# Attention with both key blocks in one set of score columns, samples' values of both heads at once, and HGRN2 sums one step behind their products

## The chip, the cores and the metric

The kernel runs on one core of a Trainium2 chip. The metric is the device time of one execution in microseconds (us), as the median of several runs. Durations inside an execution come from one profiled run.

## What is computed

One inference step of two trunk layers. There is a prompt of 1024 tokens and there are 8 samples of 8 new tokens, 1088 tokens in all, of width 1024. Each layer projects the normalised input once and feeds three mixers, of which two matter here. The reference, cut:

```python
# (A) windowed attention: 8 query heads, 2 key heads, window 128
qb_len = WINDOW if t >= WINDOW else t
k_all = jnp.concatenate([buf_k, k], axis=1)        # buf: zeros for the prompt, a cache of 128 for samples
dist = WINDOW + np.arange(qb_len)[:, None] - np.arange(kb_len)[None, :]
valid = ((dist >= 0) & (dist < WINDOW))[None] & (k_pos >= 0)[:, None, :]
s = jnp.where(valid, s, MASK_VALUE)                # s: scaled q k, per query block of 128, 256 keys
m = jnp.maximum(jnp.max(s, axis=-1, keepdims=True), sink)
p = jnp.where(valid, jnp.exp(s - m), 0.0)
denom = jnp.sum(p, axis=-1, keepdims=True) + jnp.exp(sink - m)
o = jnp.einsum('bnkgqs,bnskd->bnqkgd', p / denom, v_blk)
# (C) HGRN2: per head of 128, gate f per token and channel, k = 1 - f
#     S = f * S + k i^T ;  o = q S     (exact per-token recurrence)
```

A query t of a block sees, of the block before, the keys i > t, and of its own block the keys i <= t. For each row of 256 scores exactly 128 are therefore valid, one in each column position modulo 128.

## The kernel before

**Staging.** Per layer the kernel runs through units of two 128-column slices of the input projection. Weights and activations are split into a high and a low part, and each product is three matmuls of one pass (lines 384 to 386 for channel-major outputs in groups of 24 matmuls over 384, 384 and 320 tokens; lines 403 to 405, and 410 and 411, for token-major outputs, 24 matmuls a group). The mixers are Python generators that stand in the list `side`. After each group `group_end` calls `pump`, which moves the first two generators of the list on by one step (by three steps where `NPA` is given: the gate units during attention). What a generator emits up to its next `yield` stands in program order behind that group and ahead of the next.

**Order on the engines.** GpSimd (POOL) and SyncE (SP) run in program order (`ORDERED`). TensorE (PE), VectorE (DVE) and ScalarE (ACT) are ordered by a planner, which takes program order as priority and, with its own estimates of durations, puts a later instruction ahead where it believes the earlier one not to be ready. Semaphores then hold the real dependences.

**Attention.** `attention` interleaves, for each of 8 query blocks n, `scores(n)` (three steps) with `values(n - 1)` (three steps); for n = 0 the second place is taken by `sample_attention`. In `scores`, each group of two query heads takes four score matmuls of up to 256 columns (line 846) into a bank `sc`; one fused VectorE operation per head (line 850) adds the mask, writes `P` and keeps the row maximum. `softmax` makes exponentials in place on ScalarE (line 767, with row sums) and scales by the reciprocal (line 771). In `values`, `P` is transposed on TensorE, 128 x 128 at a time (line 867, bank `pt`), copied out (lines 870 and 872) and multiplied with the values (line 880, bank `av`, one column half of the array for each key head).

**Samples.** The values of `sample_attention` (lines 962 and 964) are, for each of 8 samples and both key heads, one matmul of 32 columns over the 128 cached keys and one over the 64 new keys; line 967 copies the result `avs` out. A full-precision matmul (all but those split ones) leaves two records in the trace, a transpose one.

**HGRN2.** Each of the 4 heads is one `hgrn` generator; at most two run side by side with the projections. It takes token pairs by levels 1, 2, 4, ... 64. For levels 0, 1 and 2 the products of query and key are made elementwise on VectorE into the tile `e` (lines 509, 532 and 560) and summed over channels by matmuls with ones into the bank `dg` (lines 518, 521, 535 and 538); the sums are then laid into `A` by VectorE (lines 527, 544, 571). From level 4 on, line 582 and its like make the products on TensorE. Between levels VectorE scales Q (line 599) and GpSimd scales K (line 600). Later steps make states and outputs (`pos`, `dss`, `ds`, `po`), normalise on GpSimd (line 713) and transpose (`yt`, line 720). In the token-major units behind the heads, `b_consts` loads the spatial weights through SP and masks them on GpSimd (lines 994 and 995).

The tiles of 1152 columns come from one pool of 17 slabs; score, transpose and sum banks from one PSUM pool of four (`paux`), the projections' banks from another of four.

Of the kernel before, what the change touches and what calls it, by code (L numbers as in the profile page):

```python
# [10 lines left out]
F32 = mybir.dt.float32  # L11
# [14 lines left out]
NEG = -1e30  # L26
# [33 lines left out]
def _consts():  # L60
# [3 lines left out]
    i = np.arange(128)  # L64
    cur = np.where(i[None, :] <= i[:, None], f(0), f(NEG))
    prev = np.where(i[None, :] > i[:, None], f(0), f(NEG))
    c["mask_p"] = np.concatenate([prev, cur], 1).astype(f)
    ms = np.full((128, 2, 192), NEG, f)
# [82 lines left out]
def build(tc, i, o, L):  # L151
# [57 lines left out]
    def late_consts():  # L209
        late["mask_p"] = cst("mask_p", [128, 256])  # L210
        late["cos"] = cst("cos", [128, 9, 8])
        late["rot"] = cst("rot", [128, 2])
        late["sin"] = cst("sin", [128, 9, 8])
        late["blk"] = cst("blk", [64, 4])
        mask_h = cp.tile([128, len(MLEV), 64], U8, tag="mask_h", name="mask_h")
        mh = slab("mh")
        nc.sync.dma_start(v3(mh[:, 0:len(MLEV) * 64], 64), i["c_mask_h"])
        V.tensor_copy(mask_h, v3(mh[:, 0:len(MLEV) * 64], 64))
        late["mask_h"] = mask_h
        mask_2 = cp.tile([128, 2, 16], U8, tag="mask_2", name="mask_2")  # L220
        nc.sync.dma_start(v3(mh[:, 512:544], 16), i["c_mask_2"])
        V.tensor_copy(mask_2, v3(mh[:, 512:544], 16))
        late["mask_2"] = mask_2

    def rsqrt(v, out, w):
# [275 lines left out]
    def hgrn(l, h, f, q, v, spill):  # L501
# [7 lines left out]
        V.tensor_mul(e[:, 0:NTOK], q[:, 0:NTOK], K[:, 0:NTOK])  # L509
        yield  # L510
        A = slab("ha")
# [19 lines left out]
        two = lambda x, n: x[:, 0:n].rearrange("p (b two) -> p b two", two=2)  # L531
        V.tensor_mul(e[:, 0:NTOK // 2], two(Q, NTOK)[:, :, 1], two(K, NTOK)[:, :, 0])
        for j in range(4):
            r, w = slice(32 * j, 32 * j + 32), slice(16 * j, 16 * j + 16)
# [17 lines left out]
        for a, m in enumerate(LEV):  # L552
# [5 lines left out]
            if m == 2:  # L558
                four = lambda x: x[:, 0:NTOK].rearrange("p (b two m) -> p b two m", two=2, m=2)
                V.tensor_mul(e[:, 0:NTOK].rearrange("p (b t s) -> p b t s", t=2, s=2),  # L560
                             four(Q)[:, :, 1, :].unsqueeze(3).to_broadcast([128, NTOK // 4, 2, 2]),
                             four(K)[:, :, 0, :].unsqueeze(2).to_broadcast([128, NTOK // 4, 2, 2]))
                pd = bank("dg2")
                group_sums(pd)
# [239 lines left out]
    def attention(l, q, kk, v, spill):  # L804
# [25 lines left out]
        def scores(n, QS):  # L830

            w = 256 if n else 128
            k0 = (n - 1) * 128 if n else 0
            P = slab("P")
            P = (P, slab("P"), 0) if n else (P, P, 512)
            st["P", n] = lambda a, g, c=0, x=w: P[a][:, a * P[2] + g * w + c:a * P[2] + g * w + c + x]
            cols = st["P", n]
            mx = small("smx", 8)
            for a in range(2):
                for gp in range(2):  # L840
                    ps = bank("sc")
                    for j in range(2):
                        g = gp * 2 + j
                        lq = QS[:, a * 512 + g * 128:a * 512 + g * 128 + 128]
                        for hl in range(2):
                            T.matmul(ps[:, j * 256:j * 256 + w], lq, KS[a][hl][:, k0:k0 + w],
                                     start=hl == 0, stop=hl == 1)
                    for j in range(2):
                        g = gp * 2 + j
                        V.tensor_tensor_reduce(cols(a, g), ps[:, j * 256:j * 256 + w],  # L850
                                               late["mask_p"][:, 256 - w:256], 1.0, -3e38, ALU.add, ALU.max,
                                               mx[:, 4 * a + g:4 * a + g + 1])
                yield
# [3 lines left out]
        def values(n):  # L857

            cols = st.pop(("P", n))
            nh = 2 if n else 1  # L860
            PT = slab("PT")
            PT = (PT, slab("PT"), 0) if n else (PT, PT, 512)
            for a in range(2):
                for hb in range(nh):
                    pt = bank("pt")
                    for g in range(4):
                        T.transpose(pt[:, g * 128:g * 128 + 128], cols(a, g, hb * 128, 128), ident)
                    d = PT[a][:, a * PT[2] + hb * 512:a * PT[2] + hb * 512 + 512]
                    if hb == 0:
                        S.copy(d, pt)  # L870
                    else:
                        V.tensor_copy(d, pt)
                yield
            del cols
            po = bank("av")
# [38 lines left out]
    def sample_attention(l, q, kn, v, spill):  # L914
# [39 lines left out]
        V.tensor_copy(PT[0:64, 512:1024], pn[0:64, :])  # L954
        yield
        po = bank("avs")
        for b in range(8):
            c, jj = b // 2, b % 2
            for a in range(2):
                s = (2 * jj + a) * 128 + 32 * c  # L960
                d = po[64 * a:64 * a + 64, b * 32:b * 32 + 32]
                T.matmul(d, cv[:, b * 128 + 64 * a:b * 128 + 64 * a + 64], PT[:, s:s + 32],
                         start=True, stop=False, tile_position=(0, 64 * a))
                T.matmul(d, v[0:64, 1024 + 64 * a:1024 + 64 * a + 64], PT[0:64, 512 + s:512 + s + 32],
                         start=False, stop=True, tile_position=(0, 64 * a))
        ys = slab("yss")
        S.copy(ys[:, 0:256].rearrange("p (g b t) -> p g b t", g=4, b=8),
               po[:, 0:256].rearrange("p (b g t) -> p g b t", b=8, g=4))
        nc.gpsimd.dma_start(spill[:, :, 1024:1088].rearrange("g p t -> p g t"), v3(ys[:, 0:256], 64))
# [421 lines left out]
```

## Time and profile before

| | before |
|---|---|
| median of 3 runs | 2421.92 us (2421.01 to 2422.5) |
| the profiled execution | 2422.11 us |
| its span in the trace | 2420.3 us |
| TensorE matmuls busy | 2345.0 us, 97% |
| TensorE weight loads busy | 2232.1 us, 92% |
| VectorE busy | 1116.6 us, 46% |
| ScalarE busy | 737.1 us, 30% |
| GpSimd busy | 398.8 us, 16% |

The span is the time from the first to the last instruction of the trace. Matmuls overlap in the pipeline, so the cost of one is read from its start to the start of the next, not from its length. A granted clock of 1.00 is TensorE at 2.4 GHz, 0.50 at 1.2 GHz; a value between is a mean over a stretch that has both.

### The profile page before, as it was taken

How to read it: one execution, taken by the hardware profiler on the slowest of the kernel's cores; microseconds unless marked ns; L12 is line 12 of the kernel's file. 1: busy time of each engine (PE TensorE's matmuls, PEld its weight loads, DVE VectorE, ACT ScalarE, POOL GpSimd, SP SyncE). 2: the span in 40 equal slices, each digit the busy share in tenths (PEclk: the TensorE clock that was granted, in tenths of full speed). 3: DMA queues.
4: the chain of work that ended last, by engine and by line, in shares of the span. 5: the costliest groups of instructions: out<-in, count | busy, mean ns of one | idle time of the engine just before them, and what ended most of it. 6: DMA issues, size and time to landing. Idle time of an engine off the chain costs nothing. (4 is left out here: it accounts for less than half of the span.)

```text
span 2420.3 us, 44177 instructions
## 1 busy us (share of the span) xinstructions
PE 2345.0 (97%) x18230; PEld 2232.1 (92%) x18230; DVE 1116.6 (46%) x2765; ACT 737.1 (30%) x1890; POOL 398.8 (16%) x429
## 2 busy tenths in 40 slices
PE   6999999989999999999999999999999999999999
PEld 5899898978899998999999998988888999999999
DVE  6446638485341232223573476476644312223251
ACT  4335632324121221212333356223332212112130
POOL 3100004242020021011110010142320101211111
PEclk9999999999999999999999999999999999999999
DMA  7421110203131233421432221111122213112141
GB/s 275 134 79 63 62 44 28 88 23 96 45 133 53 85 116 110 139 81 54 134 97 71 79 70 45 53 56 64 46 84 92 90 40 114 53 45 84 40 152 48
DMA packets 91049, 197.57 MB, mean 82 GB/s; under 512 B 14368, under 2 KB 21664, under 8 KB 90816
## 3 DMA queue, kind: packets, MB, share of 16 engines
q1 hardware_dynamic: 79616, 156.20, 19.9%
q0 software_dynamic: 11232, 38.55, 4.4%
q8 instruction: 143, 2.34, 0.4%
q14 instruction: 58, 0.48, 0.1%
HBM read 158.13 MB, written 38.54 MB: 81 GB/s over the span
## 5 line engine op out<-in xcount | busy, mean ns | idle before, releaser
L384 PE MATMUL mm<-H,wh 128*128 128x384 f32 (+1 forms) x1872 | 620.6, 331 | 2.0 <-ACT gq L1277 1.2
L386 PE MATMUL mm<-H,wh 128*128 128x384 f32 (+1 forms) x1872 | 612.9, 327 | 0.0
L385 PE MATMUL mm<-H,wl 128*128 128x384 f32 (+1 forms) x1872 | 612.4, 327 | 0.0
L403 PE MATMUL mm<-wh,H 128*128 128x256 f32 x1408 | 408.9, 290 | 0.0
L404 PE MATMUL mm<-wl,H 128*128 128x256 f32 x1408 | 401.2, 285 | 0.0
L405 PE MATMUL mm<-wh,H 128*128 128x256 f32 x1408 | 400.7, 285 | 0.0
L384 PEld LDWEIGHTS mm<-H,wh 128*128 128x128 f32 x1872 | 352.7, 188 | 16.0 <-issue 10.8
L386 PEld LDWEIGHTS mm<-H,wh 128*128 128x128 f32 x1872 | 352.3, 188 | 2.0 <-issue 1.6
L385 PEld LDWEIGHTS mm<-H,wl 128*128 128x128 f32 x1872 | 352.6, 188 | 0.3 <-issue 0.2
L339 DVE TENSOR_TENSOR wl<-wr,wh 128x512 fp32r<-128x512 f32 x308 | 219.4, 754 | 200.0 <-ACT wh L338 194.9
L403 PEld LDWEIGHTS mm<-wh,H 128*128 128x128 f32 x1408 | 271.4, 193 | 7.5 <-issue 5.2
L405 PEld LDWEIGHTS mm<-wh,H 128*128 128x128 f32 x1408 | 271.4, 193 | 2.6 <-issue 2.6
L404 PEld LDWEIGHTS mm<-wl,H 128*128 128x128 f32 x1408 | 271.8, 193 | 0.7 <-issue 0.2
L338 ACT CAST wh<-wr 128x512 fp32r<-128x512 f32 x312 | 177.7, 618 | 261.7 <-PE mm L386 204.8
L1288 DVE TENSOR_TENSOR gq<-gq,mm 128x384 f32<-128x384 f32 (+1 forms) x96 | 50.5, 531 | 336.0 <-PE mm L386 336.0
L1277 ACT ACTIVATE gq<-mm 128x384 f32<-128x384 f32 x144 | 68.1, 473 | 423.7 <-PE mm L386 403.5
L386 PE MATMUL mm<-yl,wh 128*128 128x384 f32 (+1 forms) x576 | 186.2, 330 | 5.3 <-DVE yl L1258 5.3
L384 PE MATMUL mm<-yh,wh 128*128 128x384 f32 (+1 forms) x576 | 190.3, 330 | 0.0
L385 PE MATMUL mm<-yh,wl 128*128 128x384 f32 (+1 forms) x576 | 188.4, 327 | 0.0
L1289 POOL TENSOR_TENSOR mg<-mg,gq 128x384 f32<-128x384 f32 (+1 forms) x96 | 95.4, 997 | 466.3 <-DVE gq L1288 466.3
L386 PEld LDWEIGHTS mm<-yl,wh 128*128 128x128 f32 x576 | 108.5, 189 | 6.5 <-DVE yl L1258 6.2
L1286 DVE TENSOR_TENSOR mg<-gq,mm 128x384 f32<-128x384 f32 (+1 forms) x48 | 25.1, 531 | 188.7 <-PE mm L386 120.0
(372 smaller groups left out, 3515.1 us busy)
## 6 DMA issues: line engine op xcount, KB each, us to landing
wr<-in_w_in SPq DMA_DIRECT2D x248, 256.0 KB, 3.4
wr<-in_w_ada SPq DMA_DIRECT2D x64, 256.0 KB, 3.3
yr<-y SPq DMA_DIRECT2D x24, 544.0 KB, 4.5
wr<-in_w_br SPq DMA_DIRECT2D x48, 256.0 KB, 3.2
gr<-y SPq DMA_DIRECT2D x16, 544.0 KB, 5.2
wada<-in_w_ada SPq DMA_DIRECT2D x16, 512.0 KB, 8.5
wr<-in_w_out SPq DMA_DIRECT2D x32, 256.0 KB, 3.5
y<-gq POOLq DMA_DIRECT2D x32, 192.0 KB, 2.1
```

The lines of the kernel that those rows point to most:

```text
L338: S.copy(hi, raw)
L339: eng.tensor_sub(wl[:, k0:k0 + 4, off:off + 128], raw, hi.bitcast(F32))
L384: T.matmul(ps[:, 0:n], a, rh, start=k == 0, stop=False)
L385: T.matmul(ps[:, 0:n], b, rh, start=False, stop=False)
L386: T.matmul(ps[:, 0:n], a, rl, start=False, stop=k == kk - 1)
L403: T.matmul(ps[:, 0:256], a, wh[:, k, :], start=k == 0, stop=False)
L404: T.matmul(ps[:, 0:256], a, wl[:, k, :], start=False, stop=False)
L405: T.matmul(ps[:, 0:256], b, wh[:, k, :], start=False, stop=k == 7)
L1277: S.activation(sg[c], ps, AF.Sigmoid)
L1286: V.tensor_mul(merged[j][:, t0:t0 + n], sg[c], ps)
L1288: V.tensor_mul(sg[c], sg[c], ps)
L1289: G.tensor_add(merged[j][:, t0:t0 + n], merged[j][:, t0:t0 + n], sg[c])
```

## The change

Four edits. (1) `scores`: the score matmuls stay; ScalarE copies the own block's 128 columns of two heads into `P`, VectorE overwrites those columns where the key of the block before is the valid one (a predicated copy under the mask `old`; for block 0 it puts in a large negative number), and a VectorE reduction per four heads makes the maxima. `P` has 128 columns per head where it had 256. (2) `values`: one transpose per head where there were two for n > 0; VectorE multiplies the transposed bank by the mask `oldT` for the part that goes with the values of the block before, and subtracts that from the bank for the part of the own block. The constants change accordingly: `mask_p` goes, `oldT`, `old` and a column of the negative number come. (3) `sample_attention`: one matmul of 512 columns over the new keys for all samples and both heads, then one of 64 columns per sample over its cache with the weights of both heads; the half of the output that mixes heads is not read. Four copies take the result out. (4) `hgrn`: the `yield` between the first product and the memset of `A` is taken out; one is put behind the product of line 532 and one behind that of line 560, so that their sums begin the next step.

```diff
--- before.py
+++ after.py
@@ -62,9 +62,8 @@
     c = {}
     c["ident"] = np.eye(128, dtype=f)
     i = np.arange(128)
-    cur = np.where(i[None, :] <= i[:, None], f(0), f(NEG))
-    prev = np.where(i[None, :] > i[:, None], f(0), f(NEG))
-    c["mask_p"] = np.concatenate([prev, cur], 1).astype(f)
+    c["old"] = (i[None, :] > i[:, None]).astype(f)
+    c["oldT"] = (i[:, None] > i[None, :]).astype(f)
     ms = np.full((128, 2, 192), NEG, f)
     row = np.arange(128)
     cc, t = row // 32, row % 8
@@ -207,7 +206,9 @@
     late = {}
 
     def late_consts():
-        late["mask_p"] = cst("mask_p", [128, 256])
+        late["oldT"] = cst("oldT", [128, 128])
+        late["neg"] = cp.tile([128, 1], F32, tag="neg", name="neg")
+        V.memset(late["neg"], NEG)
         late["cos"] = cst("cos", [128, 9, 8])
         late["rot"] = cst("rot", [128, 2])
         late["sin"] = cst("sin", [128, 9, 8])
@@ -221,6 +222,10 @@
         nc.sync.dma_start(v3(mh[:, 512:544], 16), i["c_mask_2"])
         V.tensor_copy(mask_2, v3(mh[:, 512:544], 16))
         late["mask_2"] = mask_2
+        old = cp.tile([128, 128], U8, tag="old", name="old")
+        nc.sync.dma_start(mh[:, 640:768], i["c_old"])
+        V.tensor_copy(old, mh[:, 640:768])
+        late["old"] = old
 
     def rsqrt(v, out, w):
         y, r = out, out.shape[0]
@@ -507,7 +512,6 @@
         V.tensor_mul(Q[:, 0:NTOK], q[:, 0:NTOK], f[:, 0:NTOK])
         e = q
         V.tensor_mul(e[:, 0:NTOK], q[:, 0:NTOK], K[:, 0:NTOK])
-        yield
         A = slab("ha")
         G.memset(A[:, 0:NTOK], 0.0)
         yield
@@ -530,6 +534,7 @@
 
         two = lambda x, n: x[:, 0:n].rearrange("p (b two) -> p b two", two=2)
         V.tensor_mul(e[:, 0:NTOK // 2], two(Q, NTOK)[:, :, 1], two(K, NTOK)[:, :, 0])
+        yield
         for j in range(4):
             r, w = slice(32 * j, 32 * j + 32), slice(16 * j, 16 * j + 16)
             T.matmul(pd[r, 288:416], ones[:, 0:32], v3(e[:, 0:512], 64)[:, :, w],
@@ -560,6 +565,7 @@
                 V.tensor_mul(e[:, 0:NTOK].rearrange("p (b t s) -> p b t s", t=2, s=2),
                              four(Q)[:, :, 1, :].unsqueeze(3).to_broadcast([128, NTOK // 4, 2, 2]),
                              four(K)[:, :, 0, :].unsqueeze(2).to_broadcast([128, NTOK // 4, 2, 2]))
+                yield
                 pd = bank("dg2")
                 group_sums(pd)
                 for j in range(4):
@@ -829,12 +835,12 @@
 
         def scores(n, QS):
 
+
             w = 256 if n else 128
             k0 = (n - 1) * 128 if n else 0
             P = slab("P")
-            P = (P, slab("P"), 0) if n else (P, P, 512)
-            st["P", n] = lambda a, g, c=0, x=w: P[a][:, a * P[2] + g * w + c:a * P[2] + g * w + c + x]
-            cols = st["P", n]
+            st["P", n] = P
+            cols = lambda a, g: P[:, (4 * a + g) * 128:(4 * a + g) * 128 + 128]
             mx = small("smx", 8)
             for a in range(2):
                 for gp in range(2):
@@ -845,33 +851,36 @@
                         for hl in range(2):
                             T.matmul(ps[:, j * 256:j * 256 + w], lq, KS[a][hl][:, k0:k0 + w],
                                      start=hl == 0, stop=hl == 1)
-                    for j in range(2):
-                        g = gp * 2 + j
-                        V.tensor_tensor_reduce(cols(a, g), ps[:, j * 256:j * 256 + w],
-                                               late["mask_p"][:, 256 - w:256], 1.0, -3e38, ALU.add, ALU.max,
-                                               mx[:, 4 * a + g:4 * a + g + 1])
+                    d = v3(P[:, (4 * a + 2 * gp) * 128:(4 * a + 2 * gp) * 128 + 256], 128)
+                    sc = v3(ps, 256)
+                    S.copy(d, sc[:, :, w - 128:w])
+                    V.copy_predicated(d, bc_mid(late["old"], 2), sc[:, :, 0:128] if n else
+                                      late["neg"].unsqueeze(2).to_broadcast([128, 2, 128]))
+                V.tensor_reduce(mx[:, 4 * a:4 * a + 4], v3(P[:, a * 512:a * 512 + 512], 128), AX.X, ALU.max)
                 yield
             softmax(lambda e: cols(e // 4, e % 4), mx, sinkp[l], 8)
             yield
 
         def values(n):
 
-            cols = st.pop(("P", n))
+            P = st.pop(("P", n))
             nh = 2 if n else 1
             PT = slab("PT")
             PT = (PT, slab("PT"), 0) if n else (PT, PT, 512)
             for a in range(2):
-                for hb in range(nh):
-                    pt = bank("pt")
-                    for g in range(4):
-                        T.transpose(pt[:, g * 128:g * 128 + 128], cols(a, g, hb * 128, 128), ident)
-                    d = PT[a][:, a * PT[2] + hb * 512:a * PT[2] + hb * 512 + 512]
-                    if hb == 0:
-                        S.copy(d, pt)
-                    else:
-                        V.tensor_copy(d, pt)
+                pt = bank("pt")
+                for g in range(4):
+                    e = (4 * a + g) * 128
+                    T.transpose(pt[:, g * 128:g * 128 + 128], P[:, e:e + 128], ident)
+                d = PT[a][:, a * PT[2]:a * PT[2] + 512]
+                if n:
+                    e = PT[a][:, 512:1024]
+                    V.tensor_mul(v3(d, 128), v3(pt, 128), bc_mid(late["oldT"], 4))
+                    V.tensor_sub(e, pt, d)
+                else:
+                    S.copy(d, pt)
                 yield
-            del cols
+            del P
             po = bank("av")
             for hb in range(nh):
                 for a in range(2):
@@ -953,19 +962,21 @@
         S.copy(PT[:, 0:512], pt)
         V.tensor_copy(PT[0:64, 512:1024], pn[0:64, :])
         yield
+
         po = bank("avs")
+        T.matmul(po, v[0:64, 1024:1152], PT[0:64, 512:1024], start=True, stop=False)
+        cols = lambda x, c, jj: x.rearrange("p (jj a c r) -> p jj a c r", jj=2, a=2, c=4)[:, jj, :, c, :]
         for b in range(8):
             c, jj = b // 2, b % 2
-            for a in range(2):
-                s = (2 * jj + a) * 128 + 32 * c
-                d = po[64 * a:64 * a + 64, b * 32:b * 32 + 32]
-                T.matmul(d, cv[:, b * 128 + 64 * a:b * 128 + 64 * a + 64], PT[:, s:s + 32],
-                         start=True, stop=False, tile_position=(0, 64 * a))
-                T.matmul(d, v[0:64, 1024 + 64 * a:1024 + 64 * a + 64], PT[0:64, 512 + s:512 + s + 32],
-                         start=False, stop=True, tile_position=(0, 64 * a))
+            T.matmul(cols(po, c, jj), cv[:, b * 128:b * 128 + 128], cols(PT[:, 0:512], c, jj),
+                     start=False, stop=b == 7)
         ys = slab("yss")
-        S.copy(ys[:, 0:256].rearrange("p (g b t) -> p g b t", g=4, b=8),
-               po[:, 0:256].rearrange("p (b g t) -> p g b t", b=8, g=4))
+        for a in range(2):
+            r = slice(64 * a, 64 * a + 64)
+            for jj in range(2):
+                d = ys[r, 0:256].rearrange("p (g c jj t) -> p jj c g t", g=4, c=4, jj=2)[:, jj]
+                x = po[r].rearrange("p (jj a c g t) -> p jj a c g t", jj=2, a=2, c=4, g=4)[:, jj, a]
+                (S.copy if jj else V.tensor_copy)(d, x)
         nc.gpsimd.dma_start(spill[:, :, 1024:1088].rearrange("g p t -> p g t"), v3(ys[:, 0:256], 64))
```

## Rows read from the trace of the kernel before

**Rows 1.** The page's first part: busy time, share of the span and instructions of TensorE.

```profile
PE 2345.0 (97%) x18230; PEld 2232.1 (92%) x18230; DVE 1116.6 (46%) x2765; ACT 737.1 (30%) x1890; POOL 398.8 (16%) x429
```

**Rows 2.** The list of waits, TensorE: line, releaser: us in total, times, longest.

```profile
PE dg L518 <- DVE q L560: 8.9, 6, 2.0
PE dg L535 <- DVE q L532: 8.4, 6, 2.4
PE yt L720 <- POOL v L713: 7.7, 6, 3.3
```

**Rows 3.** Busy time by stretch: us, then each engine (count), granted clock, DMA share, GB/s.

```profile
187.16:196.19 9.03, 9.03 (x65) 7.40 (x64) 3.51 (x7) 2.26 (x4) 0.54 (x1) 0.73 0.23 78
196.19:201.60 5.41, 5.41 (x24) 5.41 (x24) 2.58 (x10) 3.35 (x6) 0.77 (x1) 0.50 0.10 24
1383.85:1392.13 8.28, 8.28 (x65) 6.79 (x65) 3.86 (x13) 2.34 (x7) 0.54 (x1) 0.84 0.18 51
1392.13:1396.03 3.90, 3.90 (x18) 3.90 (x17) 1.91 (x4) 3.50 (x6) 0.77 (x1) 0.50 0.16 38
```

**Rows 4.** The timeline around 187 us, samples' values: start, us, engine, line, shapes, count.

```profile
187.16 0.30 PE L962 MATMUL avs<-PTs,cv 128*64 128x32 f32 x2
...
187.40 0.30 PE L964 MATMUL avs<-PTs,ts 64*64 64x32 f32 x2
```

**Rows 5.** TensorE's timeline, stretches 626 to 628 and 546 to 547 us.

```profile
626.50 1.02 PE L1003 MATMUL pz<-vb,ws 128*128 128x512 f32 x2
627.45 0.32 PE L1006 MATMUL pzs<-vb,ws 64*64 64x64 f32 x2
...
545.98 1.06 PE L685 MATMUL ds<-v,kt 128*128 128x128 f32 x8
546.87 0.38 PE L636 MATMUL pk<-c_ident,hk 128*128 128x128 f32 x2
```

**Rows 6.** TensorE's timeline, 210 to 212 us, the prompt's value products.

```profile
210.43 1.08 PE L880 MATMUL av<-PT,ts 128*64 128x512 f32 x4
211.43 1.21 PE L846 MATMUL sc<-ks,qs 128*128 128x256 f32 x8
```

**Rows 7.** TensorE's timeline, 213 to 215 us, transposes of the prompt's weights.

```profile
213.51 1.04 PE L867 MATMUL pt<-c_ident,P 128*128 128x128 f32 x8
214.30 0.39 PE L385 MATMUL mm<-H,wl 128*128 128x320 f32 x1
```

**Rows 8.** Timeline of the first head, then the stretch of three matmul groups.

```profile
348.65 1.29 DVE L509 TENSOR_TENSOR q<-q,hk 128x1088 f32<-128x1088 f32 x1
...
354.93 0.65 PE L518 MATMUL dg<-q,ones 128*32 128x256 f32 x8
...
364.17 1.28 DVE L560 TENSOR_TENSOR q<-hq,hk 128x1088 f32<-128x1088 f32 x1
...
365.51 0.66 PE L518 MATMUL dg<-q,ones 128*32 128x256 f32 x8 [0.74 <-DVE q L560]
...
343.07:354.93 11.86, 11.86 (x74) 11.67 (x73) 6.04 (x8) 5.22 (x10) 0.00 (x0) 1.00 0.29 90
```

**Rows 9.** Busy time by stretch, as in rows 3, behind a wait for `yt`.

```profile
571.47:577.14 5.67, 5.67 (x22) 4.17 (x22) 5.67 (x17) 0.69 (x1) 1.40 (x2) 0.51 0.01 3
```

**Rows 10.** VectorE's groups by line and form: count, busy us, mean ns, idle before.

```profile
L850 DVE CUSTOM_DVE_ANT_0 P<-sc,c_mask_p 128x256 f32<-128x256 f32 x112 | 42.2, 418 | 5.9 <-PE sc L846 5.5
...
L872 DVE COPY PT<-pt 128x512 f32<-128x512 f32 x28 | 19.3, 688 | 8.0 <-PE pt L867 8.0
...
L544 DVE COPY_PREDICATED ha<-mask_h,dg 32x128 f32<-32x128 uint8 x32 | 14.0, 439 | 0.7
...
L737 DVE TENSOR_REDUCE rss<-rq 64x8 f32<-64x512 f32 x2 | 1.3, 670 | 0.0
```

**Rows 11.** Busy time by stretch, as in rows 3, the fullest slice of attention.

```profile
230.00:240.00 10.00, 9.99 (x72) 9.47 (x71) 9.36 (x27) 5.93 (x11) 1.08 (x2) 1.00 0.21 67
```

**Rows 12.** ScalarE's groups by line: count, busy us, mean ns, idle before.

```profile
L767 ACT ACTIVATE P<-P,snm 128x256 f32<-128x256 f32 (+1 forms) x128 | 61.7, 485 | 21.0 <-DVE snm L761 12.5 <-DVE ses L763 8.5
```

## The prediction

> **What bounds the kernel now.** I read the busy shares first: TensorE's matmuls cover 97% of the span, its weight loads nearly as much [rows 1]. The reader sees that no other engine is near that, so an edit counts by the TensorE time that it takes away, or by the idle time of TensorE that it closes; work of VectorE and ScalarE counts only where TensorE waits for it. Next the list of TensorE's waits [rows 2]: in HGRN2, `dg` products of line 518 wait 8.9 us for the product `e` of line 560, those of line 535 wait 8.4 us for line 532, and the transposes `yt` wait 7.7 us for GpSimd's scaling. The attention's scores and values wait so little that the list does not name them. Last the stretches in which the granted clock is at its lower level [rows 3, 9]: two of them begin inside the samples' value products, one behind a `yt` wait.
>
> **Samples' values.** Before, 32 small matmuls a layer (lines 962 and 964, two records each); their stretch takes 9.03 us in the first layer and 8.28 us in the second [rows 3], together 17.3 us. Each costs 0.24 us at the full clock although it has only 32 columns [rows 4]. In both stretches the clock falls from the 2.4 to the 1.2 GHz level part of the way (mean 0.73 and 0.84), and the work behind them runs at 0.50 for 5.41 and 3.90 us before it rises again [rows 3].
> After: one matmul of 512 columns and eight of 64 columns with 128x128 weights. The nearest price of the first is line 1003, 0.95 us from its start to the next line's [rows 5]. For the eight, four matmuls of 128 columns with full weights take 0.89 us, 0.22 each [rows 5]; those of 32 columns cost 0.24, so 64 columns should lie there too. That makes 0.95 + 8 x 0.22 = 2.7, of which overlap at the seams takes a little: 2.6 us a layer, bounds 2.1 (each of the eight at some 0.14, were the columns to count) and 3.5. Saved: 17.3 - 5.2 = 12.1 us. As dense work of 2.6 us follows and precedes full-rate matmuls I take it that the clock stays up; half of 5.41 + 3.90 us is 4.65 us more. Term: -16.8 us, and -10 if the clock falls all the same.
> The four evacuations in place of one (two on VectorE, two on ScalarE) come behind the last matmul and feed a DMA to DRAM that is read much later; I cost them at nothing.
> A rule of the Trainium skill speaks against this part: "TensorE: Matmul & The Clock Gate", Part 3 on packing small matmuls, says that outputs in different column groups run side by side, which full-width outputs give up. The rows of the prompt's values agree with it: two half-width matmuls of 512 columns take 1.00 us, as one full-width does [rows 5, 6]. The samples' rows do not: 0.24 us for each [rows 4]. Were they packed they would cost as 16, 3.8 us a layer, and the term without the clock would be 2.4 us; the measured stretch decides.
>
> **Prompt's values.** Both key blocks are now in one set of 128 columns, so a block n > 0 transposes 8 tiles and not 16. Per layer 7 x 8 = 56 transposes go, 112 in all. Eight take 0.79 us to the next line's start, 0.099 each [rows 7]. Term: -11.1 us, all of it on TensorE's path. The score products and the value products keep their count (the two masked halves of the transposed tile go in separately).
>
> **What the scores and values now ask of VectorE and ScalarE.** Removed: 112 fused mask-and-maximum operations of 256 columns, 42.2 us, and 28 copies, 19.3 us [rows 10], 61 us (block 0's 16 shorter ones left out). Added on VectorE: 64 predicated copies of 256 elements; the nearest row has 128 elements in 0.44 us [rows 10], so 0.44 to 0.88, 28 to 56 us; 32 reductions of 512 elements at 0.67 [rows 10], 21 us; 28 products and 28 differences of 512 elements out of PSUM at the 0.69 of the copy, 39 us. Net +27 to +55 us, less what the shorter scaling gives back. ScalarE gets 64 copies of 256 columns, loses 28 of 512, and its exponentials have half as many columns. In the busiest slice VectorE already works 9.36 of 10 us while TensorE loses nothing [rows 11], because other projections stand between the steps. I put +2 us of new waits here; 0 if the gaps hold it all, +20 if they do not.
> The constants add one load on SP's queue, ahead of the modulation weights, and a cast: at most +1, taken as 0.
>
> **HGRN2's order.** A step of a head is emitted after each group of 24 projection matmuls. Two steps are added (the products `e` of lines 532 and 560 now end a step, their sums begin the next) and one is removed (GpSimd's memset joins the first step). What the trace shows of the old order: line 560's product starts at 364.17 and takes 1.28 us, TensorE stands for 0.74 us and then begins line 518 at 365.51 [rows 8]. With a group between (three take 11.86 us [rows 8], so 4.0 us each) each wait of at most 2.4 us [rows 2] is covered. The removed step hits the first sums: line 509's product ends at 349.94, line 518 begins at 354.93 [rows 8], 5.0 us of slack; one group earlier leaves 1.0. At heads whose vector work is denser less is left, so I keep 4 us of the 17.3 us (8.9 + 8.4): term -13.3, bounds -4 and -17.3. TensorE's order is made by a planner that fills in projection matmuls where it believes a product to be late; where it already did, the yield changes little, hence the lower bound.
> One step more per head also moves the ends of the heads. In the old order the third head's normalisation falls just behind the spatial masks, whose products GpSimd makes; `yt` waits up to 3.3 us for line 713 [rows 2], and behind that TensorE runs 5.67 us at 0.51 [rows 9]. Counting the steps, that head's scaling is now emitted two groups after the masks. If so some 2.2 us of wait and half of 5.67 us go per layer, 10 us in all; as the order of the queues could bring it back I count 6. Against it stands the fourth head's state load: it is emitted after the masks' loads and the next weights on SP, so its users may wait 0 to 2 us per layer: +1.
> The heads still end in the second unit of `ub`, ahead of the point where all side work is run out, and by the count of tiles no more than 17 slabs are alive, as before.
>
> **Sum.** -16.8 - 11.1 + 2 - 13.3 - 6 + 1 = -44.2 us. The profiled execution took 2422.1 us (span 2420.3), the median of the runs is 2421.9, so they agree: 2377.9 us, 1.8% less.
>
> **Rivals.** A, VectorE binds in attention: for it speaks the slice at 9.36 of 10 [rows 11], against it that TensorE's list names neither `sc` nor `pt` nor `av`. Price 10 to 20 us: 2388 to 2398. B, the planner puts the sums back where they wait: what speaks for it is that the trace has sums standing amid a group, not at its end; only some 4 us of term -13.3 is kept, 2387, and with the `yt` wait kept too 2393. C, slower: the score banks are now freed only after a ScalarE copy, and that copy may stand behind a burst of eight exponentials, 8 x 0.485 = 3.9 us [rows 12]; the next scores then find no bank. At 3.9 us for each of 16 blocks that is +62 us, 2439; it decides the sign from 44.2 / 16 = 2.8 us a block. Against it: the exponentials get shorter, four banks serve, and the projections have banks of their own. "TensorE: Matmul & The Clock Gate" of the Trainium skill calls ScalarE's queue strict first-in first-out (its section on the 32x32 sub-arrays), which is what C needs; no row here shows a copy behind such a burst holding TensorE. D, better: the waits of HGRN2's `yt` all go, none come new, and predicated copies are cheap: -16.8 - 11.1 - 17.3 - 10 = -55.2, 2367, and with the samples' lower bound and a shorter first `yt` wait some 4 us less, 2363.
>
> **How the numbers follow.** Forecast 0.47 (its own range 2370 to 2386), A 0.2, B 0.15, D 0.1, C 0.05, and 0.03 for a sum of small losses that ends within 0.2% of before (some 5 us, about what a measurement tells from none). Leaving out C and the tails of A and D, the range is 2363 to 2399. Faster 0.92, same 0.03, slower 0.05.
>
> **What would show it.** After: a samples' value stretch near 2.6 us with the clock at 1.00 behind it; 128 `pt` transposes, not 240; line 518's and 535's waits under 5 us in all; `yt` under 4 us and no lower clock behind it; VectorE's busy time up by 20 to 55 us without a new wait of TensorE on `sc`, `pt` or `av`. Wrong it is made by waits on these three tiles, or by sums that wait for line 509 or 532.

## The result and the profile after

The changed kernel takes 2384.2 us (median; 2382.2 to 2388.0) against 2422.2 us: 0.9846 of the time before, 95% interval 0.9829 to 0.9863. That is 38 us less where the forecast was 44 less (2377.9), inside the range, with the sign as forecast. The profiled execution, the shortest of the four, took 2382.2 us with a span of 2380.1, which is 40.2 us under the span of before. Where terms are added up below, it is done against spans.

The page's first part answers [rows 1]:

```profile
PE 2310.4 (97%) x18026; PEld 2200.4 (92%) x18026; DVE 1121.3 (47%) x2639; ACT 730.8 (31%) x1928; POOL 396.4 (17%) x429
```

TensorE is still the bound. Of the 40.2 us, 34.6 left its busy time (2345.0 to 2310.4) and 5.6 its idle time (span less busy: 75.3 to 69.7). The forecast had it otherwise: it looked for some 16 of its 44 us in waits that end, and put in 3 us for new ones.

The list of TensorE's waits, answering [rows 2] (line, releaser: us in total, times, longest):

```profile
PE dg L522 <- DVE q L514: 6.1, 2, 3.0
...
PE dg L540 <- DVE q L536: 5.2, 2, 2.6
...
PE pts L959 <- DVE Ps L777: 3.2, 2, 1.6
PE yt L726 <- POOL v L719: 2.9, 2, 1.5
PE ds L691 <- DVE s L683: 2.7, 2, 1.6
PE dg L522 <- DVE q L565: 2.2, 2, 1.4
```

Line 522 is line 518 of before, 540 is 535, 726 is 720. Three waits are new. The first sums of a head (line 522, product of line 514) stand once in each layer for 3.0 us: this is where the removed step struck. The samples' transposes (line 959) wait 1.6 us a layer for the samples' softmax. And the products `ds` of line 691 wait 2.7 us in all for VectorE's addition to the state (line 683). By the code they read nothing that line 683 writes; that they wait for a PSUM bank that it reads is likely, but no run shows it. None of the three attention tiles that the forecast feared (`sc`, `pt`, `av`) is listed.

The stretches that answer [rows 3] and [rows 9] (us, then each engine's busy time with its count, granted clock, DMA share, GB/s):

```profile
188.81:191.69 2.88, 2.88 (x20) 2.12 (x20) 2.34 (x11) 2.81 (x8) 0.00 (x0) 1.00 0.00 0
191.69:196.00 4.31, 4.31 (x33) 4.28 (x32) 4.15 (x9) 3.53 (x9) 1.31 (x2) 1.00 0.35 100
1364.50:1367.40 2.90, 2.90 (x19) 2.14 (x20) 1.88 (x10) 2.83 (x10) 0.00 (x0) 1.00 0.00 0
...
571.00:577.00 6.00, 6.00 (x54) 6.00 (x53) 0.30 (x1) 2.60 (x13) 0.54 (x1) 1.00 0.13 50
370.30:372.30 2.00, 2.00 (x9) 2.00 (x9) 1.93 (x8) 0.00 (x0) 0.00 (x0) 0.51 0.00 0
1672.90:1676.30 3.40, 3.40 (x44) 3.11 (x43) 3.24 (x8) 2.56 (x6) 1.32 (x2) 0.52 0.01 2
```

The samples' values take 2.88 and 2.90 us in place of 9.03 and 8.28, with the clock at 1.00 (the 2.4 GHz level) in and behind them. In the timeline the wide product (line 967) takes 1.06 us to the start of the next line, and the eight narrow ones (line 971) 1.83 us, 0.23 each:

```profile
188.75 1.12 PE L967 MATMUL avs<-PTs,ts 64*128 64x512 f32 x2
189.81 2.00 PE L971 MATMUL avs<-PTs,cv 128*128 128x64 f32 x16
191.64 0.61 PE L824 MATMUL pq<-c_ident,tq 128*128 128x128 f32 x4
```

The stretches of 5.41 and 3.90 us at half clock are gone, and so is the one near 571 us behind `yt`. The last two rows are new: they stand behind the new 3.0 us wait of line 522 and the 2.6 us wait of line 540.

VectorE's and ScalarE's groups that answer [rows 10] and [rows 12] (count, busy us, mean ns, idle before):

```profile
L857 DVE COPY_PREDICATED P<-old,sc 128x256 f32<-128x256 uint8 x56 | 22.6, 439 | 2.7 <-ACT P L856 2.5
L859 DVE TENSOR_REDUCE smx<-P 128x4 f32<-128x512 f32 x32 | 21.8, 680 | 0.4
L878 DVE TENSOR_TENSOR PT<-pt,c_oldT 128x512 f32<-128x512 f32 x28 | 19.1, 684 | 4.5 <-PE pt L874 4.5
L879 DVE TENSOR_TENSOR PT<-pt,PT 128x512 f32<-128x512 f32 x28 | 18.9, 682 | 0.1
...
L773 ACT ACTIVATE P<-P,snm 128x128 f32<-128x128 f32 x128 | 49.6, 389 | 9.7 <-DVE snm L767 5.6 <-DVE ses L769 3.9
```

A predicated copy of 256 elements takes 439 ns, as one of 128 elements did [rows 10]: the lower of the two bounds.

### The profile page after: what moved, and what is told of

The parts are those of the page before. It is cut to its first block, busy times and chain, and to the rows that moved or that the text cites. A ratio compares the mean times of both kernels' runs of the same rounds, so it can differ in the third digit from the quotient of the medians.

```text
span 2380.1 us, 43687 instructions
## 1 busy us (share of the span) xinstructions
PE 2310.4 (97%) x18026; PEld 2200.4 (92%) x18026; DVE 1121.3 (47%) x2639; ACT 730.8 (31%) x1928; POOL 396.4 (17%) x429
## 4 chain that ended last, share of the span: by engine, by line
PE 71%; issue 12%; DVE 11%; DMA 2%; ACT 2%; POOL 2%; SPq 0%; POOLq 0%; DVEq 0%; ACTq 0%
PE mm L389 16%; PE mm L391 15%; PE mm L390 15%; PE mm L408 4%; PE mm L410 3%; PE mm L409 3%; PE mm L1347 2%; PE mm L1349 2%; PE mm L1348 2%; DVE wl L344 1%; PE av L889 1%; PE sc L852 1%; DVE yl L1269 1%; DVE ha L577 1%; PE ada L290 1%
```

## Experiments

All times are medians; each ratio is to the kernel before run beside it, which took 2420.1 to 2421.0 us beside e1 to e12. Page figures (span, TensorE busy, the difference as idle) are of the profiled execution.

| kernel | us | ratio, 95% interval | span | busy | idle |
|---|---|---|---|---|---|
| before | 2422.2 | 1 | 2420.3 | 2345.0 | 75.3 |
| changed | 2384.2 | 0.983 to 0.986 | 2380.1 | 2310.4 | 69.7 |
| e1 attention alone | 2397.2 | 0.989 to 0.992 | 2395.9 | 2319.6 | 76.3 |
| e2 HGRN2 alone | 2414.5 | 0.997 to 0.998 | 2412.6 | 2348.2 | 64.4 |
| e3 first cut back | 2380.3 | 0.982 to 0.986 | 2376.6 | 2310.7 | 65.9 |
| e4 samples alone | 2407.3 | 0.993 to 0.996 | 2404.3 | 2330.7 | 73.6 |
| e5 scores alone | 2413.2 | 0.996 to 0.998 | 2410.0 | 2331.8 | 78.2 |
| e6 samples split | 2419.9 | 0.998 to 1.000 | 2419.6 | 2344.6 | 75.0 |
| e7 samples reordered | 2411.2 | 0.994 to 0.997 | 2411.2 | 2338.5 | 72.7 |
| e8 samples later | 2382.6 | 0.983 to 0.986 | 2379.8 | 2311.4 | 68.4 |
| e9 second cut only | 2385.4 | 0.984 to 0.987 | 2382.5 | 2309.4 | 73.1 |
| e10 third cut only | 2383.0 | 0.983 to 0.986 | 2383.1 | 2313.2 | 69.9 |
| e11 cut at the end | 2376.9 | 0.981 to 0.984 | 2376.1 | 2309.3 | 66.8 |
| e12 first level joined | 2388.2 | 0.986 to 0.989 | 2384.5 | 2313.6 | 70.9 |

"Cut" is a `yield` in `hgrn`, where a head's work is broken off until the next group of projections.

### Which part brings what: e1, e2, e4, e5

e1 is the changed kernel with the three HGRN2 edits undone, e2 the kernel before with these three alone, e4 with the samples' values alone, e5 with the prompt's scores and values alone.

> The attention edits alone, HGRN2 as before. Theory: the parts add up on TensorE's path. Samples' values 11.5 us less matmul time and 4.7 us of lower clock, 112 transposes 11 us, against that 3 us of a new wait of the samples' transposes pts for line 771's scaling: about 2422 - 24 = 2398 us, with dg waits of 17 us as in the kernel before. Rival: the new order of HGRN2 brings nothing, then this kernel takes about the 2384 us of the changed one. The pts wait of 1.6 us a layer should stand here too if the attention edits make it.

> The three moved yields alone, attention as before. Theory: about -9 us of idle time of TensorE in HGRN2 and -3 to -6 us of lower clock behind the old yt wait: 2408 to 2412 us; the wait of line 518 for line 509 of about 3 us a layer appears here too, and no wait of pts. Rival: the planner puts the sums back where they waited: 2418 to 2422 us.

> Only the samples' values of both heads at once, all else as before. Theory: 9 new matmuls take 2.9 us in place of 9.03 and 8.28, and the clock stays at 1.00 behind them: 2422 - 11.5 - 4.7 = 2406 us. Rival: the clock falls there for another reason and only the matmul time goes: 2410.5 us. No pts wait.

> The kernel before with the prompt's scores and values of the change alone (samples' values and HGRN2 sums as before). Theory: 112 transposes of 0.099 us leave TensorE (-11.1 us), and the samples' transposes now wait for their softmax, 1.6 us in each layer (+3.2 us): 2413 us against 2421. The samples' value stretches stay 9.0 and 8.3 us with a granted clock under 0.9. Rival: the wait at the samples' transposes belongs to the samples' own edit (then it is not seen here, and the time is 2410).

e1, e4 and e5 came out within 2 us of what their first theory said. The attention is worth 24 us. e4 saved 13.7 us against the kernel before run beside it, about midway between 16.2 with the clock term and 11.5 without, so its time does not tell the two apart. Its trace does: the clock stays at 1.00 in and behind the samples' products in both layers.

```profile
188.00:200.00 12.00, 11.60 (x78) 10.52 (x78) 10.10 (x29) 6.66 (x13) 1.85 (x3) 1.00 0.35 113
1376.00:1394.00 18.00, 18.00 (x116) 15.99 (x116) 12.31 (x42) 12.54 (x38) 1.85 (x3) 1.00 0.27 87
```

e5 shows the wait of line 959's kind, 3.2 us, and e4 does not: it belongs to the prompt's scores, whose work on VectorE and ScalarE pushes back the samples' softmax; the rival is out.

e2 missed by 2.5 us. Its idle time fell by 10.9 us but its busy time rose by 3.2 with the same instructions: the mean granted clock of the run is 0.989, that of before 0.992. On top of the attention edits the same three cuts bring 13.0 us (2397.2 to 2384.2), and 9.2 of 15.8 us in the spans are busy time. So the cuts act on the clock as much as on the waits, and not always to the good. One can add up what the lower clock takes over a whole trace: from 40 us on, in stretches of 2 us, each length times what the granted clock lacks of 1.00. That is 20.5 us before, 25.6 in e2, 15.4 in e1 and 5.5 in the changed kernel.

### The removed cut: e3, e8, e12

The changed kernel with the cut behind the first product put back. By the count of live tiles a head can't have two steps more than before without a further slab, so in each of these runs another cut leaves: in e3 that between the second and third group of key transposes.

```diff
         V.tensor_mul(e[:, 0:NTOK], q[:, 0:NTOK], K[:, 0:NTOK])
+        yield
...
-            yield
+            if u0 != 4:
+                yield
```

> The changed kernel with the yield behind the first product put back, and the one between the second and third group of key transposes taken out in its place, so that a head has as many steps as in the changed kernel. Theory: the taken yield caused the wait of 3.0 us a layer of the first sums for line 514; it goes, with the lower clock behind it: 2384 - 6 to -9, so 2375 to 2378 us. Rival: the planner's lateness moves to the next sums, 2382 to 2386 us.

2380.3, by the medians half of the expected gain. The two ratios are only 0.0007 apart and their intervals overlap, so even that half is not clear of the noise. In the list of e3's waits line 522's 6.1 us are gone, but others stand in their place:

```profile
PE yt L728 <- POOL v L721: 4.4, 4, 1.5
PE lvs L602 <- DVE ha L578: 4.1, 4, 1.4
PE lv L599 <- DVE hq L606: 4.0, 2, 2.0
...
PE lv L599 <- DVE ht L608: 3.2, 2, 1.6
```

e8 adds one step between the samples' softmax and their transposes:

```diff
         softmax(lambda s: P[:, s * 192:s * 192 + 192], mx, sinks[l], 4)
         yield
+        yield
```

> The changed kernel with the first sums one group later again and the cut between the second and third group of key transposes left out (as in the run of that edit before), and with one more step between the samples' softmax and their transposes, so that the samples' transposes and values come one step of the prompt later. Theory (the transposes wait only because the softmax in front of them now ends later on VectorE and ScalarE): the waits of 1.6 us at the samples' transposes go, about -3 us: 2377 us, against 2380 for that edit without it and 2384 for the changed kernel. Rival: the later step meets another wait (the samples' values for the copy of the transposed scores, or the slab that is now held longer): 2380 or more.

The wait at the samples' transposes is gone from e8's list, but `sc` (2.0 us) and `pt` (1.1) have entered it, and the time is no shorter than e3's: the rival held.

e12 puts the cut back too and joins the first level to the second sums instead of the key transposes:

```diff
-            yield
+            if a:
+                yield
```

> The changed kernel with the cut behind the first product put back, and the cut ahead of the first level left out in its place (that level has no matmuls, so TensorE's order hardly moves, and a head has as many groups as in the changed kernel). Theory (the changed kernel lost 6 us at the first sums of the second head because that cut was taken out): this wait goes and no wait at the level products takes its place, unlike in the run where the key transposes were joined: 2374 to 2379 us. Rival (the waits of a head only change place as its groups move): 2380 to 2385.

2388.2, 3 us beyond even the rival's range. Line 522's wait on the first product went, and the level products `lv` now wait 9.1 us for line 607. That the first sums' wait goes was right both times; that its 6 us are gained was not: other waits stood at later steps.

### Is it the separation of product and sums? e9, e10, e11

Each is e1 plus one single cut, so a head has one step more than before: e9 behind the second product, e10 behind the third, e11 at the very end of the head, where it separates nothing.

```diff
+        yield
         nc.gpsimd.dma_start(spill[h], yc[:, 0:NTOK])
```

> The changed kernel with two of its three HGRN2 edits undone: the first sums are a group later again and the third sums follow their product at once, as before; only the cut behind the second product stays. So it is the run of the attention edits alone (2397.2) plus one cut. Theory 1 (each cut pays its own wait and no more): of the waits of the second sums (8.5 us in the run without the cut) 2 to 2.6 us stay, the third sums keep their 6.6 us: 2391 us. Theory 2 (what helps is that a head is spread over one more group, so that the rescaling transposes at yt and the level products at lv fall too, 13.0 us there): 2383 to 2387.

> As the run with the cut behind the second product alone, with the cut behind the third product in its place: the second sums follow their product at once and keep their 8.5 us, the third sums' 6.6 us fall to about 2. Theory 1 (each cut pays its own wait): 2392 to 2393 us. Theory 2 (one more group for each head, whichever): 2383 to 2387.

> The run of the attention edits alone (2397.2 us) plus one cut that separates no product from its sums: it stands behind the last transposes of a head, ahead of the DMA that stores it. Theory A (any cut that makes a head one group longer moves the later heads against the group boundaries, and that is what shortened the waits and took the lower clock away): 2383 to 2387 us. Theory B (the cut has to fall between a product and the matmuls that read it, or at least before the levels): the waits of the second and third sums keep their 15 us and the time is 2395 to 2399.

2385.4, 2383.0 and 2376.9. Each cut alone brings what all three edits together brought, and the one that separates nothing brings most: 20.3 us beyond e1, and 5 to 7 us less than the changed kernel (by the ratios and by the medians). The theory that each cut pays for its own wait is out as an account of the time, though for the waits themselves it held in e9, where the second sums' fell to 2.6 us and the third sums' stayed at 6.9. With the attention edits in, one more step for each head was enough at each of the three places tried; e11 came out 6 us below even the range of its theory A. It is no general price: e3 and e12 have one step more as well and differ by 8 us, and on the kernel before the three edits together gave 6.5 us. The end cut on the kernel before was not run.

e11's list still has most of the waits of the second sums, which the change meant to remove, while those of `yt` and of the third sums fell without a cut of their own:

```profile
PE dg L540 <- DVE q L537: 7.5, 6, 1.8
...
PE yt L725 <- POOL v L718: 3.2, 4, 1.1
...
PE dg L523 <- DVE ht L606: 1.8, 4, 0.5
PE dg L523 <- DVE q L565: 1.5, 2, 0.8
```

In e1 these stood at 8.5, 7.2 and 6.6 us. From e1 to e11, with the same instructions, 9.5 us leave the idle and 10.3 us the busy time. The second figure is the clock: added up as above, it takes 15.4 us in e1 and 3.5 in e11. (In e9 it takes 3.4, and 10.2 of e9's 13.4 us in the spans are busy time.) Three of e1's stretches at the lower level:

```profile
501.90:505.00 3.10, 3.10 (x16) 3.10 (x16) 1.57 (x4) 0.41 (x1) 3.02 (x2) 0.50 0.04 8
558.20:563.40 5.20, 5.20 (x20) 3.70 (x20) 5.20 (x16) 0.69 (x1) 0.93 (x2) 0.51 0.00 2
1742.00:1747.10 5.10, 5.10 (x25) 4.93 (x24) 5.10 (x18) 0.00 (x0) 0.94 (x1) 0.50 0.00 2
```

The first follows a 2.41 us wait of the fourth head's second sums, the second and third waits of 3.0 us at `yt`. In e11, whose longest wait on these lines is 1.8 us, the like stretches are at full clock:

```profile
501.50:505.00 3.50, 3.50 (x32) 3.50 (x31) 3.46 (x9) 1.92 (x8) 0.20 (x1) 1.00 0.07 11
550.00:579.50 29.50, 28.38 (x245) 26.93 (x238) 10.78 (x44) 10.00 (x42) 8.02 (x6) 1.00 0.15 52
```

Why a wait shrinks when a head merely moves can be seen at the third head's third sums. In e1 (start, us, engine, line, shapes; VectorE, then GpSimd, then TensorE):

```profile
470.28 0.72 DVE L537 TENSOR_TENSOR q<-hq,hk 128x544 f32<-128x544 f32 x1
471.27 2.13 DVE L604 TENSOR_TENSOR hq<-hq,f 128x544 f32<-128x544 f32 x1
...
471.08 1.73 POOL L605 TENSOR_TENSOR hk<-hk,f 128x544 f32<-128x544 f32 x1 [4.69 <-DVE q L537]
...
476.77 0.66 PE L523 MATMUL dg<-q,ones 128*32 128x256 f32 x8 [1.67 <-DVE q L565]
```

and the same operations in e11:

```profile
473.72 0.72 DVE L537 TENSOR_TENSOR q<-hq,hk 128x544 f32<-128x544 f32 x1
474.50 0.72 DVE L604 TENSOR_TENSOR hq<-hq,f 128x544 f32<-128x544 f32 x1
...
474.53 2.15 POOL L605 TENSOR_TENSOR hk<-hk,f 128x544 f32<-128x544 f32 x1 [8.30 <-DVE q L537]
...
478.61 0.66 PE L523 MATMUL dg<-q,ones 128*32 128x256 f32 x8 [0.46 <-DVE ht L606]
```

In both, a small VectorE product of another step (line 606) stands between lines 537 and 604. In e1 it took 0.43 us, so GpSimd began 0.19 us ahead of line 604, and VectorE's product there took 2.13 us. In e11 it took 0.22, VectorE began 0.03 us ahead, and line 604 took 0.72. The 1.4 us lie in the chain of the third product, and TensorE's wait for it falls from 1.67 to 0.46. This is shown for this wait. That it is the rule is not: e9 and e10 have 2.13 us there and gain all the same. A full account of the 20 us by place stays open.

### The samples' value products: e6, e7

e6 is the kernel before with the 32 small products cut into two halves, other work between them:

```diff
         for b in range(8):
+            if b == 4:
+                yield
             c, jj = b // 2, b % 2
```

> The kernel before with one edit: the samples' value matmuls (all 32, unchanged) are cut in two halves with other work put between them. Theory (an unbroken stretch of these small matmuls is what the lower clock follows): the matmul time stays 0.24 us for each pair, the granted clock stays at 1.00 in and behind both halves, about -4.6 us: 2416 to 2417 us against 2421. Rival (the clock falls for another reason, or it falls in each half): no change, 2421.

No gain. e6's stretches:

```profile
186.21:189.89 3.68, 3.68 (x34) 3.03 (x33) 2.86 (x6) 1.74 (x3) 0.29 (x1) 1.00 0.02 4
190.49:193.38 2.89, 2.89 (x14) 2.89 (x14) 1.65 (x6) 2.37 (x5) 0.00 (x0) 0.50 0.48 147
204.00:208.02 4.02, 4.02 (x35) 3.23 (x32) 3.00 (x11) 1.65 (x6) 0.61 (x1) 0.89 0.13 49
208.02:214.03 6.01, 6.01 (x27) 5.95 (x27) 2.25 (x9) 1.66 (x3) 0.77 (x1) 0.51 0.10 25
```

Behind each half stands a stretch at half clock (the 1.2 GHz level). Halving the unbroken row of these products does not save the clock; the theory is out.

e7 keeps the 32 products and changes their order: the two heads' cached products side by side, then their own ones.

```diff
-            for a in range(2):
...
+            for own in range(2):
+                for a in range(2):
...
+                    if own:
...
+                    else:
...
```

> The kernel before with the same 32 samples' value matmuls in another order: the two heads' cached products side by side (left and right half of the output rows), then the two heads' own products, where before each head's cached and own product stood together. Theory A (neighbours into different halves of the array's columns overlap, as the pairs of the prompt's values do in the trace of before): the stretch falls from 8.3 to 9.0 us to about 4.5 us in each layer, and with the lower clock behind it gone the time is 2408 to 2413 us. Theory B (matmuls of 32 columns cost their fixed time whatever the order): 0.24 us each stays and the time is 2421.

2411.2, as theory A had it: 9.6 us for an order alone.

```profile
188.06:192.00 3.94, 3.94 (x65) 3.33 (x65) 3.15 (x5) 2.58 (x5) 0.54 (x1) 1.00 0.02 4
...
1377.51:1381.66 4.15, 4.15 (x62) 3.47 (x63) 3.86 (x13) 2.19 (x7) 0.33 (x1) 0.84 0.00 0
1382.43:1387.36 4.93, 4.93 (x21) 4.93 (x20) 3.93 (x12) 2.67 (x4) 0.50 (x1) 0.52 0.34 113
```

The first window begins a little late and takes in 0.4 us of the next line; in the timeline the 32 products run from 187.73 to 191.52, in the second layer from 1377.19 to 1381.34. 3.79 us are 0.12 each, half of [rows 4]. Neighbours of one kind that write different halves of the output rows overlap. In the order of before none did: from product to product it is 0.23 to 0.24 us at the full clock throughout, also where the own product of one head is followed by the cached one of the other, in the other half. No run tells what in the change of kind stops the overlap. The lower clock went in the first layer and stayed in the second, so what sets it off remains open.

## Why the forecast was right, and where it was off

**Samples' values, -16.8: right.** The rows of after give 17.31 - 5.78 = 11.5 and 4.65 for the clock, 16.2; e4 alone saved 13.7 by the medians, 16.0 in the spans. A stretch takes 2.9 us, not 2.6: the wide product takes 1.06 where the forecast had 0.95, the eight narrow ones cost 0.23 each, between its two rows of 0.22 and 0.24, and nothing overlaps at the seams. It weighed the packing rule of the Trainium skill ("TensorE: Matmul & The Clock Gate", Part 3) and set it aside on the row of 0.24 us. e7 shows that the rule holds here and that the order had kept it from acting; the forecast's own 3.8 us a layer for packed products is what e7's first layer took. The wide form is still shorter, 2.9 us against 3.8 and 4.15, and by the medians e4 is 4 us ahead of e7 (2407.3 against 2411.2), though their intervals overlap. The term had no entry for this cheaper edit of the order alone, worth 9.6 of the samples' 13.7 us.

**Transposes, -11.1: right.** The page after lists 128 of them; e5's 7.6 us are these less the 3.2 us wait, to within 0.4.

**New waits in attention, +2: 3.2 measured, at a place not named.** The forecast looked at `sc`, `pt` and `av`; the wait is at the samples' transposes. VectorE's busy time grew by 4.7 us only, not 20 to 55. With the attention edits alone it grew by 16.1 (1116.6 to 1132.7); 11.4 left in HGRN2, where the products of lines 604 and 605 stand against GpSimd less often (15 of 56 over 0.95 us in the changed kernel, 27 in e1).

**HGRN2's sums, -13.3, and `yt` with its clock and the state load, -6 + 1: 18.3 together, 13.0 measured (15.8 in the spans).** The time is near, but the parts were wrong. The failed step is "with a group between each wait of at most 2.4 us is covered". The `dg` waits on VectorE fell from 17.3 to 13.5 us, by 3.8 and not by 13.3, just short of the lower bound of 4, and by the forecast's own sign (sums that wait for line 509 or 532) this part is wrong: the second head's first sums wait 3.0 us a layer, and the fourth head's second sums still wait 2.6. For the first head the slack that the forecast read did stay (line 514 ends at 336.34, its sums begin at 337.82). At the second head VectorE comes to the product late, and takes 2.07 us for it where 1.29 is the median of the eight, while GpSimd works at line 606 from 365.75 to 367.83 (VectorE, then TensorE):

```profile
366.91 2.07 DVE L514 TENSOR_TENSOR q<-q,hk 128x1088 f32<-128x1088 f32 x1
...
365.52 0.42 PE L389 MATMUL mm<-H,wh 128*128 128x320 f32 x1
365.78 0.31 PE L390 MATMUL mm<-H,wl 128*128 128x320 f32 x1
369.12 1.10 PE L522 MATMUL dg<-q,ones 128*32 128x256 f32 x8 [3.04 <-DVE q L514]
369.95 0.36 PE L525 MATMUL dg<-q,ones 128*32 128x32 f32 x4
370.24 0.64 PE L391 MATMUL mm<-H,wh 128*128 128x320 f32 x1
```

TensorE's order let two projection matmuls of the group pass ahead of the sums and kept the others of that group behind them. The 2.6 us wait has the same form: two matmuls of a group, then sums whose product VectorE began only at 1670.29. Since the first sums' matmuls had ended at 1664.3 it had been busy without a gap, largely for the other head, for 6 us where a group takes 4.0. The forecast counted the length of the product and not the work that stands ahead of it on VectorE.

What the forecast gave the smaller share, that one step more moves the ends of the heads, is by e11 enough by itself. `yt` did as forecast: 7.7 to 2.9 us, and no lower clock near 571 us. And half clock behind waits, which the forecast counted for `yt` alone (some 3 of its 6 us), counted elsewhere as well: 9.2 of the 15.8 us are busy time. That these made up for the waits that stayed is luck, as e2 shows: without the attention edits the same three edits gave 6.5 us. No wait for the state load is listed; the wait of 2.7 us at `ds`, which no term had, is.

**Sum.** From -44.2 to -40.2: HGRN2 2.5 us less by the spans, the attention's wait 1.2, the samples 0.6; the three make 4.3, where 4.0 is measured.

**Rivals.** A: no wait on its tiles, out. B came nearest: sums do wait for lines 514 and 536, amid a group, and of the term of 13.3 us only 3.8 came, as B had it; its 2387 us is nearer to 2384.2 than the forecast's 2377.9. But the planner did not move them ahead of the group that the new cut put between; it let too few matmuls of the next group pass them; for line 514 the removed cut is the condition, since no run with that cut has the wait. The clock gained much of what the waits kept. C: no score product is in the list of waits. D: the waits of `yt` went mostly, those of the sums did not.

## What to carry to other kernels

In a kernel whose side work is fed into the gaps of one bounding engine, a cut in that work also moves everything behind it: try the same cut where it separates nothing before you credit its place. Before small matmuls are merged into a wide one, try to put neighbours of one kind into different halves of the output rows. And price a wait of 2 to 3 us on TensorE with the work behind it that may run at the 1.2 GHz level: from e1 to e11 that was worth as much as the waits.

## What the runs showed of the hardware

VectorE and GpSimd hold each other up where both read their operands from SBUF. VectorE's product of 544 columns took 0.72 us where it led by 0.03 us and 2.13 where GpSimd led by 0.19; GpSimd's took 2.15 and 1.73. "SBUF — State Buffer" of the Trainium skill (section "Who interferes with whom") says that the two share a port pair, that a VectorE instruction with two SBUF inputs contends for it with a GpSimd instruction that reads SBUF, and that the pair is an exclusive lock. VectorE's times agree with it: in e1 its product ended 0.59 us after GpSimd's, a little under its own length of 0.72. The start alone does not always tell who is held up: in e9 line 605 began at 478.02, 0.35 us ahead of GpSimd's line 606, and still took 2.33 us; GpSimd was issuing a DMA when it began.

The half clock behind a wait is not a fixed price: waits of 2.4 and 3.0 us in e1 and of 3.0 and 2.6 us in the changed kernel had it behind them, for 2 to 5 us, but a wait of 2.4 us in e9, at the third sums of the fourth head, was followed by the stretch at the full clock shown below. Nor does it take a wait: in the kernel before the clock fell inside the samples' products, where TensorE was busy for all of the 9.03 us [rows 3]. The stretch of e9:

```profile
509.30:512.50 3.20, 3.20 (x92) 2.88 (x91) 3.15 (x8) 0.92 (x5) 1.36 (x1) 1.00 0.39 143
```
